# Seven-product pairs with the sums on VectorE and low parts of slabs by accumulating transfers

## The chip, the core and the metric

The kernel runs on one core of a Trainium2 chip. The engines that matter here are TensorE (PE, which multiplies, with PEld for its weight loads), VectorE (DVE), ScalarE (ACT), GpSimd (POOL) and SyncE (SP, which issues the loads). Each works through its own list of instructions in order and waits at semaphores for the others. The metric is the device time of one execution in microseconds.

## What is computed

One decoder layer over 512 tokens with 1024 features: half a feed-forward layer, a mixer of two recurrent branches, half a feed-forward layer, and a normalisation. All in float32.

```python
D_MODEL = 1024
SEQ = 512
D_FF = 2816

def swiglu(x, w_in, w_out):
    a, b = jnp.split(x @ w_in, 2, axis=-1)
    return (jax.nn.silu(a) * b) @ w_out

h = h + 0.5 * swiglu(rmsnorm(h, ffn1_norm[l]), ffn1_w_in[l], ffn1_w_out[l])
h = h + hybrid_mixer(rmsnorm(h, mix_norm[l]), ...)
h = h + 0.5 * swiglu(rmsnorm(h, ffn2_norm[l]), ffn2_w_in[l], ffn2_w_out[l])
```

The change touches the two feed-forward layers alone.

## The kernel before

**Three matmuls for one.** A product in full float32 precision is made of three matmuls in the faster float32r type: each operand is split into a rounded high part and the rest, the low part, and `mm3` (lines 166 to 169) adds high times high, high times low and low times high in PSUM. For a slab of weights (128x512, 256 KB) ACT casts the loaded tile to the high part `whi` (line 298), and DVE subtracts the high part from the tile to get the low part `wlo` (line 282).

**A stream of units.** A feed-forward layer is a list of units, one slab of 12 matmuls each, that `stream` lays out by hand, in the order in which each engine shall run them. After the matmuls of unit t it emits, for later units, the low part of unit t+5, the sums for unit t+8, the cast of unit t+6, and the loads for which a buffer has come free. `WB = 6` buffers hold high and low parts, so the cast for unit t+6 waits until PE is done with unit t. Raw slabs lie in three buffers `raw` or, in the stage described next, in six buffers `rw`; a count of readers (`left`) in the program tells when the next load may be put into SP's list (line 275).

**Pairs.** The hidden layer has 2816 columns, 22 blocks of 128. A pair is one block of `a` and the block of `b` that it is multiplied with. In the plain form a pair is eight products, four units of full-width matmuls (512 columns each; tiles `pmm`), two for `a` and two for `b`. In the seven-product form (`fast`, from line 315) the eight quarter products of the 2x2 blocked matrices are replaced by seven, in the scheme of Strassen and Winograd: seven units of half-width matmuls (256 columns; tiles `px`), of which three take a loaded tile as it is (`a11`, `a12`, `a22`), and four take a sum `sw` of loaded tiles (`s1` to `s4`, made at line 327 on POOL). The results come together on DVE in `fa`, `uu`, `uc` (line 346) and `vb` (line 362), ACT takes the silu, and the gate multiplies both halves (line 426). Results of the last five blocks are split again at once (lines 429 and 430).

**Before the stage** the normalised input has to be put into seven operands `xs` with high and low parts (`operands`, from line 387): eight scalings on DVE (line 399), four differences on POOL and DVE (line 398), seven casts on ACT (line 396) and seven low parts on DVE (line 397). They are spread over ten units from unit 2 (first layer) or 3 (second layer) on. PE meanwhile does pairs in the plain form: two in units 0 to 7 of the first layer, whose first two pairs are done in an opening, and three in units 0 to 11 of the second. So 18 and 19 of the 22 pairs are made in the seven-product form.

**Behind it** comes the output product, eight columns of six units each (`w2`), with the split of the gated blocks (lines 485 and 486) in its first column.

The mixer's order is made by a planner of its own and is not touched.

Of the kernel before, what the change touches and what calls it, by code (L numbers as in the profile page):

```python
# [8 lines left out]
F32 = mybir.dt.float32  # L9
# [3 lines left out]
ALU = mybir.AluOpType  # L13
# [3 lines left out]
P = 128  # L17
T = 512
NT = T // P
D = 1024  # L20
KD = D // P
# [18 lines left out]
WB = 6  # L40
RW, SW = 6, 4
# [84 lines left out]
def body(tc, xT, cst, sqc, hmask, dta, w1o, w1a, w2a, wt, wn, wab, wbh, wbg, wo, w1b, w2b, yT, dbg=None):  # L126
# [110 lines left out]
    class Unit:  # L237

        def __init__(self, raws, operand, run, comb=None, drop=()):
            self.raws, self.operand, self.run, self.comb, self.drop = raws, operand, run, comb, drop  # L240

    def plain(src, nk, xs, where, n=T):
# [3 lines left out]
        def unit(k):  # L246
# [9 lines left out]
            return Unit([raw], lambda: raw.tile[:, :w_ * P], run, drop=(raw,))  # L256
        return [unit(k) for k in range(0, nk, 4)], held

    def stream(units, fp, early, hooks, posts):
# [18 lines left out]
        def ahead(comb, cast, low):  # L278
            while todo["low"] < min(low, len(units)):
                i = todo["low"]  # L280
                x, hi, lo = parts[i]
                dve.tensor_tensor(lo, x, hi.bitcast(F32), op=ALU.subtract)  # L282
                for r in units[i].drop:
                    r.left -= 1
                todo["low"] += 1
# [6 lines left out]
            while todo["cast"] < min(cast, len(units)):  # L292
# [5 lines left out]
                act.copy(hi, x)  # L298
                parts[i] = x, hi, lo
# [6 lines left out]
        for t, u in enumerate(units):  # L306
# [5 lines left out]
            ahead(min(t, todo["cast"]) + WB + 3, min(t + WB + 1, todo["cast"] + 2), min(t + WB, todo["cast"]))  # L312
        assert not waiting

    def fast(w, p, xo, fp, at, posts, gate):
# [7 lines left out]
        def comb(n, x, y, op):  # L323
            def f():
                a, b = (z.tile if isinstance(z, Raw) else v[z] for z in (x, y))
                v[n] = fp.tile([P, T], F32, name="sw", bufs=SW)
                pool.tensor_tensor(v[n], a, b, op=op)  # L327
# [45 lines left out]
        for t, f in ((0, f0), (2, f2), (3, f3), (4, f4), (6, f6), (7, f7), (8, f8)):  # L373
# [5 lines left out]
            Unit([a11, a21], raw(a11), prod(0, 0, "m"), drop=(a11,)),  # L379
            Unit([a22, a12], of("s2"), prod(2, 0, "a"), lambda: (s1(), s2())),  # L380
            Unit([], raw(a12), prod(3, 1), drop=(a12,)),
# [3 lines left out]
            Unit([], raw(a22), prod(6, 0), drop=(a22,))]  # L385

    def operands(c0, xs, rooms, start, hooks):
# [4 lines left out]
              for o in range(7)]  # L392
# [8 lines left out]
        work = ((scaled(0), scaled(1)), (scaled(2), scaled(3), less(pool, t1, b12, b11)),  # L401
                (high(0), scaled(4), scaled(5)), (scaled(6), scaled(7), low(0)),
                (less(pool, b12, b22, b12), less(dve, t2, b22, t1), high(3), high(2)), (low(2), low(3), high(1)),
                (low(1), less(pool, t2, b21, t2), high(4)), (low(4), high(5)), (low(5), high(6)), (low(6),))
# [4 lines left out]
    def ffn(w1, w2, c0, after, slow, lead=None, last=None):  # L409

        with tc.tile_pool(name="ff", bufs=1) as fp, \
# [33 lines left out]
            if lead is not None:  # L445
# [4 lines left out]
                for p in range(2):  # L450
                    f = columns([lambda x=x: x for x in pts[2 * p:2 * p + 2]], ("fa", "uc"), p, *([pool, dve][p],) * 2)
# [7 lines left out]
            for p in range(done, slow):  # L459
                us = []  # L460
                for n in range(2):
                    x, held = plain(w1[ORDER[p], n], KD, ux, pa if lead is None and p == 0 else mm)
# [39 lines left out]
            for d in range(KD if last is None else KD - 1):  # L502
                x, held = plain(w2[d], KF, lambda k, d=d: go[k] if d < 2 else moved[k], mm)
# [125 lines left out]
    ffn(w1a, w2a, C_F1, nextnorm(C_MX, hd, defer=True), 4, lead=lead)  # L629
# [1304 lines left out]
```

## Time and profile before

| what | us |
|---|---|
| median of 3 runs | 1681.99 (1681.3 to 1683.33) |
| profiled execution | 1681.47 |
| its span, first to last instruction | 1679.7 |
| PE busy in the span | 1617.8 |
| DVE busy | 1266.9 |
| POOL busy | 572.0 |
| first layer, seven-product matmuls | 56.8 to 271.4 |
| second layer, seven-product matmuls | 1327.6 to 1543.4 |

The busy time of PE is modelled from the starts of pipelined matmuls, so a busy PE may still run below its best rate; the number of matmuls in a stretch tells that rate. A timeline row gives start, duration, engine, line, operation, output and inputs, and in brackets the idle time ahead of it with what ended that. Instructions of one engine overlap by some 0.08 us in the rows, so the time from start to start is a little shorter than the duration.

### The profile page before, as it was taken

How to read it: one execution, taken by the hardware profiler on the slowest of the kernel's cores; microseconds unless marked ns; L12 is line 12 of the kernel's file. 1: busy time of each engine (PE TensorE's matmuls, PEld its weight loads, DVE VectorE, ACT ScalarE, POOL GpSimd, SP SyncE). 2: the span in 40 equal slices, each digit the busy share in tenths (PEclk: the TensorE clock that was granted, in tenths of full speed). 3: DMA queues.
4: the chain of work that ended last, by engine and by line, in shares of the span. 5: the costliest groups of instructions: out<-in, count | busy, mean ns of one | idle time of the engine just before them, and what ended most of it. 6: DMA issues, size and time to landing. Idle time of an engine off the chain costs nothing.

```text
span 1679.7 us, 29400 instructions
## 1 busy us (share of the span) xinstructions
PE 1617.8 (96%) x10708; PEld 1395.8 (83%) x10708; DVE 1266.9 (75%) x2212; ACT 768.9 (46%) x1779; POOL 572.0 (34%) x782
## 2 busy tenths in 40 slices
PE   9799989999999999999999999999999899999997
PEld 8698988888888888887888888888888798988787
DVE  5999999345778859757889887755544999999534
ACT  5344446334335245536766565554234443445322
POOL 1655542000221212056617656600001655542001
PEclk9899999999999999999999999999999999999999
DMA  6133332334223223453334234445633233332333
GB/s 199 45 96 92 91 100 77 117 117 125 72 62 95 53 82 95 124 151 103 95 105 119 86 110 127 130 150 176 199 109 105 88 96 90 95 95 73 102 100 113
DMA packets 107425, 178.70 MB, mean 106 GB/s; under 512 B 19584, under 2 KB 25472, under 8 KB 107280
## 3 DMA queue, kind: packets, MB, share of 16 engines
q1 hardware_dynamic: 106992, 176.60, 35.3%
q8 instruction: 84, 1.38, 0.3%
q14 instruction: 61, 0.50, 0.1%
q10 hardware_dynamic: 288, 0.22, 0.0%
HBM read 161.80 MB, written 14.97 MB: 105 GB/s over the span
## 4 chain that ended last, share of the span: by engine, by line
PE 69%; DVE 24%; issue 4%; ACT 2%; DMA 1%; SPq 0%; POOL 0%; DVEq 0%; POOLq 0%; ACTq 0%
PE pmm L167 18%; PE pmm L169 17%; PE pmm L168 17%; DVE wlo L282 11%; DVE rooma L426 3%; DVE roomb L426 2%; PE pnat L167 2%; PE pnat L169 2%; PE pnat L168 2%; DVE uc L346 1%; DVE uu L346 1%; DVE fa L346 1%; DVE g L426 1%; DVE xs L397 1%; PE pog L1357 1%
## 5 line engine op out<-in xcount | busy, mean ns | idle before, releaser
L167 PE MATMUL pmm<-uh,whi 128*128 128x512 f32 (+1 forms) x863 | 358.6, 416 | 3.1 <-DVE uc L440 3.1
L169 PE MATMUL pmm<-uh,wlo 128*128 128x512 f32 (+1 forms) x863 | 337.8, 391 | 0.0
L168 PE MATMUL pmm<-ul,whi 128*128 128x512 f32 (+1 forms) x863 | 336.5, 390 | 0.0
L169 PE MATMUL px<-xs,wlo 128*128 128x256 f32 x1036 | 301.3, 291 | 30.1 <-DVE wlo L282 29.9
L167 PE MATMUL px<-xs,whi 128*128 128x256 f32 x1036 | 296.6, 286 | 7.9 <-DVE fa L440 4.2
L168 PE MATMUL px<-xs,whi 128*128 128x256 f32 x1036 | 296.6, 286 | 5.3 <-DVE xs L397 5.3
L1711 DVE TENSOR_TENSOR wlo<-raw,whi 128x512 fp32r<-128x512 f32 x226 | 157.9, 699 | 118.5 <-ACT whi L1709 116.9
L1709 ACT CAST whi<-raw 128x512 fp32r<-128x512 f32 x226 | 140.3, 621 | 224.7 <-PE pmm L168 177.4
L169 PEld LDWEIGHTS px<-xs,wlo 128*128 128x128 f32 x1036 | 201.7, 195 | 39.5 <-DVE wlo L282 39.3
L167 PEld LDWEIGHTS px<-xs,whi 128*128 128x128 f32 x1036 | 201.9, 195 | 8.9 <-ACT xs L396 6.3
L168 PEld LDWEIGHTS px<-xs,whi 128*128 128x128 f32 x1036 | 201.9, 195 | 6.4 <-DVE xs L397 6.4
L169 PEld LDWEIGHTS pmm<-uh,wlo 128*128 128x128 f32 x863 | 162.4, 188 | 36.0 <-DVE wlo L558 0.2
L167 PEld LDWEIGHTS pmm<-uh,whi 128*128 128x128 f32 x863 | 162.9, 189 | 33.2 <-issue 3.5
L168 PEld LDWEIGHTS pmm<-ul,whi 128*128 128x128 f32 x863 | 163.1, 189 | 28.6 <-DVE ul L194 0.3
L327 POOL TENSOR_TENSOR sw<-rw 128x512 f32<-128x512 f32 x74 | 120.4, 1627 | 151.0 <-DMA rw<-w1b 60.5
L282 DVE TENSOR_TENSOR wlo<-raw,whi 128x512 fp32r<-128x512 f32 x122 | 95.5, 797 | 88.6 <-ACT whi L298 88.1
L282 DVE TENSOR_TENSOR wlo<-sw,whi 128x512 fp32r<-128x512 f32 x148 | 146.8, 1010 | 0.0
L298 ACT CAST whi<-raw 128x512 fp32r<-128x512 f32 x122 | 71.7, 590 | 145.8 <-PE pmm L168 85.1
L205 POOL TENSOR_TENSOR acc<-acc,sqt 128x512 f32<-128x512 f32 x18 | 23.5, 1304 | 321.6 <-ACT sqt L203 321.6
L282 DVE TENSOR_TENSOR wlo<-rw,whi 128x512 fp32r<-128x512 f32 x111 | 97.6, 880 | 0.0
L167 PE MATMUL pmm<-xs,whi 128*128 128x512 f32 (+1 forms) x238 | 90.1, 379 | 3.0 <-ACT xs L485 3.0
L168 PE MATMUL pmm<-xs,whi 128*128 128x512 f32 (+1 forms) x238 | 90.2, 379 | 1.7 <-DVE xs L486 1.7
(478 smaller groups left out, 3315.6 us busy)
## 6 DMA issues: line engine op xcount, KB each, us to landing
raw<-wt SPq DMA_DIRECT2D x160, 256.0 KB
rw<-w1b SPq DMA_DIRECT2D x76, 256.0 KB
rw<-w1a SPq DMA_DIRECT2D x72, 256.0 KB
raw<-w2b SPq DMA_DIRECT2D x45, 256.0 KB
raw<-w2a SPq DMA_DIRECT2D x40, 256.0 KB
raw<-wn SPq DMA_DIRECT2D x32, 256.0 KB
raw<-wbg SPq DMA_DIRECT2D x32, 256.0 KB
gb<-gtd SPq DMA_DIRECT2D x16, 256.0 KB
```

The costliest lines, as they stand in the source:

```text
L167: pe.matmul(pt, ah, bh, start=first, stop=False)
L168: pe.matmul(pt, ah, bl, start=False, stop=False)
L169: pe.matmul(pt, al, bh, start=False, stop=last)
L205: add.tensor_tensor(acc, acc, s, op=ALU.add)
L282: dve.tensor_tensor(lo, x, hi.bitcast(F32), op=ALU.subtract)
L298: act.copy(hi, x)
L327: pool.tensor_tensor(v[n], a, b, op=op)
L346: dve.tensor_tensor(t2, p2, add.to_broadcast([P, 2, 256]) if twice else add, op=ALU.add)
L397: low = lambda o: lambda: dve.tensor_tensor(xo[o][1], what[o], xo[o][0].bitcast(F32), op=ALU.subtract)
L426: mul.tensor_tensor(g[:, c], x, y, op=ALU.mult)
L1709: act.copy(hi, raw)
L1711: dve.tensor_tensor(lo, raw, hi.bitcast(F32), op=ALU.subtract)
```

## The change

1. The four sums of a pair (`sw`) move from POOL to DVE, and so do POOL's three differences in `operands` and, in the first layer, the scaling and gate of the pair from the opening.
2. A unit may be marked `fold`. Its low part is then not made on DVE: ACT writes minus the high part into `wlo`, and POOL issues a transfer that reads the slab from memory a second time and adds it onto `wlo` on arrival. Marked are the three plain tiles of each seven-product pair, the units of the eight-product pairs from the fourth block of the first layer and the second of the second layer on, and the first output column of each layer.
3. The sums are emitted one unit later (`COMB = 2` where 3 stood).
4. The first layer makes one pair more in eight products (`slow` is 5, was 4), so 17 and 19 pairs are left in the seven-product form.

```diff
-RW, SW = 6, 4
+RW, SW, COMB = 6, 4, 2
...
-            return Unit([raw], lambda: raw.tile[:, :w_ * P], run, drop=(raw,))
+            return Unit([raw], lambda: raw.tile[:, :w_ * P], run, drop=(raw,), fold=raw.src if fold else None)
...
                 x, hi, lo = parts[i]
-                dve.tensor_tensor(lo, x, hi.bitcast(F32), op=ALU.subtract)
-                for r in units[i].drop:
-                    r.left -= 1
+                if units[i].fold is None:
+                    dve.tensor_tensor(lo, x, hi.bitcast(F32), op=ALU.subtract)
+                    for r in units[i].drop:
+                        r.left -= 1
                 todo["low"] += 1
...
                 act.copy(hi, x)
+                if units[i].fold is not None:
+
+                    act.mul(lo, hi.bitcast(F32), -1.0)
+                    pool.dma_start(lo, units[i].fold, accum_op=ALU.add)
+                    for r in units[i].drop:
+                        r.left -= 1
...
-            ahead(min(t, todo["cast"]) + WB + 3, min(t + WB + 1, todo["cast"] + 2), min(t + WB, todo["cast"]))
+            ahead(min(t, todo["cast"]) + WB + COMB, min(t + WB + 1, todo["cast"] + 2), min(t + WB, todo["cast"]))
...
-                pool.tensor_tensor(v[n], a, b, op=op)
+                dve.tensor_tensor(v[n], a, b, op=op)
...
-            Unit([a11, a21], raw(a11), prod(0, 0, "m"), drop=(a11,)),
+            Unit([a11, a21], raw(a11), prod(0, 0, "m"), drop=(a11,), fold=a11.src),
...
-        work = ((scaled(0), scaled(1)), (scaled(2), scaled(3), less(pool, t1, b12, b11)),
+        work = ((scaled(0), scaled(1)), (scaled(2), scaled(3), less(dve, t1, b12, b11)),
...
-                    f = columns([lambda x=x: x for x in pts[2 * p:2 * p + 2]], ("fa", "uc"), p, *([pool, dve][p],) * 2)
+                    f = columns([lambda x=x: x for x in pts[2 * p:2 * p + 2]], ("fa", "uc"), p, dve, dve)
...
-                    x, held = plain(w1[ORDER[p], n], KD, ux, pa if lead is None and p == 0 else mm)
+                    x, held = plain(w1[ORDER[p], n], KD, ux, pa if lead is None and p == 0 else mm, fold=p > (2 if lead is not None else 0))
...
-                x, held = plain(w2[d], KF, lambda k, d=d: go[k] if d < 2 else moved[k], mm)
+                x, held = plain(w2[d], KF, lambda k, d=d: go[k] if d < 2 else moved[k], mm, fold=d == 0)
...
-    ffn(w1a, w2a, C_F1, nextnorm(C_MX, hd, defer=True), 4, lead=lead)
+    ffn(w1a, w2a, C_F1, nextnorm(C_MX, hd, defer=True), 5, lead=lead)
```

What the engines' lists then hold. First DVE, one seven-product pair in the first layer, before (lines as in the profile; `x2` is a row that comes twice):

```order
L282 TENSOR_TENSOR wlo<-rw,whi 128x512
L346 TENSOR_TENSOR fa<-px,p_874 128x512
L282 TENSOR_TENSOR wlo<-rw,whi 128x512
L282 TENSOR_TENSOR wlo<-sw,whi 128x512
L346 TENSOR_TENSOR uu<-px,fa 128x512
L362 TENSOR_TENSOR vb<-px,uu 128x256
L282 TENSOR_TENSOR wlo<-rw,whi 128x512
L282 TENSOR_TENSOR wlo<-sw,whi 128x512
L346 TENSOR_TENSOR uc<-px,uu 128x512
L282 TENSOR_TENSOR wlo<-sw,whi 128x512 x2
L426 TENSOR_TENSOR roomb<-fa,uc 128x256
L426 TENSOR_TENSOR roomb<-uc,vb 128x256
```

And DVE in such a pair of the changed kernel, up to the first of the gate's two rows (later lines have moved by up to seven; L334 is the sum, L283 the low part, L353 and L369 the results, L433 the gate):

```order
L334 TENSOR_TENSOR sw<-rw 128x512
L334 TENSOR_TENSOR sw<-sw,rw 128x512
L353 TENSOR_TENSOR fa<-px,p_1268 128x512
L283 TENSOR_TENSOR wlo<-sw,whi 128x512
L353 TENSOR_TENSOR uu<-px,fa 128x512
L369 TENSOR_TENSOR vb<-px,uu 128x256
L334 TENSOR_TENSOR sw<-rw 128x512
L283 TENSOR_TENSOR wlo<-sw,whi 128x512
L334 TENSOR_TENSOR sw<-rw,sw 128x512
L353 TENSOR_TENSOR uc<-px,uu 128x512
L283 TENSOR_TENSOR wlo<-sw,whi 128x512 x2
L433 TENSOR_TENSOR rooma<-fa,uc 128x256
```

The three low parts of loaded tiles are gone, and four sums stand in their places; each sum is for a unit of the next pair.

ACT in the same pair before, from the silu of `uc` to the next:

```order
L368 ACTIVATE uc<-uc 128x256
L351 COPY p_874<-px 128x256
L298 CAST whi<-rw 128x512 x2
L298 CAST whi<-sw 128x512
L357 ACTIVATE fa<-fa 128x256
L298 CAST whi<-rw 128x512
L298 CAST whi<-sw 128x512 x3
```

And in the changed kernel (L302 writes minus the high part):

```order
L375 ACTIVATE uc<-uc 128x256
L358 COPY p_970<-px 128x256
L299 CAST whi<-rw 128x512
L302 ACTIVATE wlo<-whi 128x512
L299 CAST whi<-rw 128x512
L302 ACTIVATE wlo<-whi 128x512
L299 CAST whi<-sw 128x512
L364 ACTIVATE fa<-fa 128x256
L299 CAST whi<-rw 128x512
L302 ACTIVATE wlo<-whi 128x512
L299 CAST whi<-sw 128x512 x3
```

Each cast of a loaded tile is followed by the product by -1 that starts from it.

POOL at the start of the first layer, in the changed kernel (before, its list held the sums of L327 here, four a pair):

```order
L230 ISA
L230 TENSOR_TENSOR rcol<-msq,mhalf 128x4
L303 DMA wlo<-w1a 128x512 x59
L303 DMA wlo<-w2a 128x512 x5
L303 DMA wlo<-w2a 128x256
L508 CAST roomb<-uh 128x512
```

POOL issues 65 transfers in the first layer (8 for eight-product pairs, 51 for 17 seven-product pairs, 6 for the output column) and nothing else between the norm and the copies behind the first output column.

14 lines of the change are left out of this document (7 added, 7 removed).

## The prediction

> **What bounds the kernel now.** I first read the page: busy shares and the 40 slices (42 us each).
>
> ```profile
> PE 1617.8 (96%) x10708; PEld 1395.8 (83%) x10708; DVE 1266.9 (75%) x2212; ACT 768.9 (46%) x1779; POOL 572.0 (34%) x782
> ...
> DVE  5999999345778859757889887755544999999534
> ...
> POOL 1655542000221212056617656600001655542001
> PEclk9899999999999999999999999999999999999999
> ```
>
> PE at 96% hides two stretches, slices 2 to 7 and 32 to 37, where DVE stands at 9 and POOL works beside it: the seven-product stages of the two feed-forward layers. Next the same stretch by windows (PE, PEld, DVE, ACT, POOL busy, then clock, DMA share and GB/s).
>
> ```profile
> core 0: us, PE busy (x) PEld busy (x) DVE busy (x) ACT busy (x) POOL busy (x), PEclk, DMA share, GB/s
> 40.00:60.00 20.00, 15.47 (x68) 12.72 (x66) 19.51 (x17) 4.87 (x8) 13.61 (x7) 0.90 0.14 44
> 60.00:80.00 20.00, 13.61 (x76) 12.53 (x77) 19.45 (x18) 10.56 (x17) 12.12 (x6) 0.76 0.17 51
> 80.00:100.00 20.00, 20.00 (x167) 19.88 (x166) 19.96 (x24) 8.25 (x18) 10.76 (x8) 1.00 0.31 83
> 100.00:120.00 20.00, 19.12 (x159) 18.86 (x157) 19.93 (x23) 8.64 (x19) 12.38 (x8) 1.00 0.31 92
> 0.00:20.00 20.00, 18.95 (x84) 15.97 (x85) 14.30 (x25) 15.30 (x27) 0.20 (x4) 1.00 0.79 259
> 108.00:109.00 1.00, 0.93 (x8) 0.73 (x7) 1.00 (x1) 0.00 (x0) 0.87 (x1) 1.00 0.45 133
> 109.00:110.00 1.00, 0.19 (x1) 0.19 (x2) 1.00 (x3) 0.00 (x0) 0.00 (x0) 1.00 0.34 129
> ```
>
> From 80 us on DVE has no gap (19.93 of 20), while PE loses almost a microsecond at 109. Before that, at 40 to 80 us, PE stands idle for 11 us and its clock drops to 0.76. So VectorE sets the pace. Third, DVE in order of time over one pair, and what POOL does then (start, duration):
>
> ```profile
> 109.07 0.68 DVE L282 TENSOR_TENSOR wlo<-rw,whi 128x512 fp32r<-128x512 f32 x1
> 109.67 0.68 DVE L346 TENSOR_TENSOR fa<-px,p 128x512 f32<-128x512 f32 x1
> ...
> 112.19 0.42 DVE L362 TENSOR_TENSOR vb<-px,uu 128x256 f32<-128x256 f32 x1
> 112.53 0.68 DVE L282 TENSOR_TENSOR wlo<-rw,whi 128x512 fp32r<-128x512 f32 x1
> 113.13 1.79 DVE L282 TENSOR_TENSOR wlo<-sw,whi 128x512 fp32r<-128x512 f32 x1
> ...
> 117.42 1.52 DVE L426 TENSOR_TENSOR roomb<-fa,uc 128x256 f32<-128x256 f32 x1
> 118.86 1.51 DVE L426 TENSOR_TENSOR roomb<-uc,vb 128x256 f32<-128x256 f32 x1
> 120.29 0.68 DVE L282 TENSOR_TENSOR wlo<-rw,whi 128x512 fp32r<-128x512 f32 x1
> ...
> 265.81 0.42 DVE L426 TENSOR_TENSOR g<-fa,uc 128x256 f32<-128x256 f32 x1
> ```
>
> ```profile
> 112.52 1.85 POOL L327 TENSOR_TENSOR sw<-rw 128x512 f32<-128x512 f32 x1 [3.65 <-DMA rw<-w1a]
> ...
> 116.97 1.68 POOL L327 TENSOR_TENSOR sw<-rw 128x512 f32<-128x512 f32 x1 [0.63 <-DVE wlo L282]
> ```
>
> A pair takes 120.29 - 109.07 = 11.22 us. The same 128x512 subtraction takes 0.68 us (0.60 from start to start) without POOL and 1.79 us beside POOL's sum; the 128x256 product of the gate takes 1.52 us beside POOL and 0.42 us (0.34 from start to start) at 265.81, after POOL's last sum. DVE is full because POOL's reads hold up its instructions with two SBUF inputs.
>
> **The change, part by part.** *DVE in the steady pair.* Three subtractions go, four sums come, and POOL's reads end. Left are 11 instructions of 128x512 at 0.60 and three of 128x256 at 0.34: 6.6 + 1.0, and 0.1 for the wait between `uu` and `vb`, 7.7 us in place of 11.22. The sums have two SBUF inputs as the subtractions do, so I take 0.60; were they as slow as beside POOL (1.79) DVE would need 12.5, which gives 1613 + 36 x 2.4 = 1700 us by the sum below. I keep that as the far end, though nothing is left that would make them so.
>
> *PE is then late next.* Its spacing from rows:
>
> ```profile
> 37.91 0.39 PE L169 MATMUL pmm<-uh,wlo 128*128 128x512 f32 x1
> ...
> 52.19 0.39 PE L169 MATMUL pmm<-uh,wlo 128*128 128x512 f32 x1
> 56.79 0.55 PE L167 MATMUL px<-xs,whi 128*128 128x256 f32 x1 [4.22 <-DVE fa L440]
> ...
> 82.08 0.28 PE L167 MATMUL px<-xs,whi 128*128 128x256 f32 x1
> ...
> 84.00 0.28 PE L168 MATMUL px<-xs,whi 128*128 128x256 f32 x1
> ...
> 1292.10 1.05 PE L221 MATMUL pbc<-sq,rcol 128*128 128x128 f32 x8
> ```
>
> 64 full-width matmuls from 37.91 up to 52.42 give 0.227 us each, so a unit of 12 takes 2.72 and an eight-product pair (48) 10.88; 16 half-width ones from 82.08 to 84.00 give 0.120, so a unit takes 1.44 and a seven-product pair (84) 10.08. The ends of both stages:
>
> ```profile
> L169 PE MATMUL px<-xs,wlo x504: 278/283/582, 57.4 to 271.3; 128*128 128x256 f32 x168
> L169 PE MATMUL px<-xs,wlo x532: 277/283/581, 1328.0 to 1543.3; 128*128 128x256 f32 x178
> ```
>
> First layer: the eight-product pairs end at 52.42 and the stage of 18 pairs at 271.42. With one pair more in eight products: 52.42 + 10.88 + 17 x 10.08 = 234.7, a gain of **36.7 us**. Second layer: unit 2 starts behind the `pbc` matmuls, at 1292.10 + 1.05 = 1293.2; ten units later, at 1320.4, the 19 pairs could start, and end at 1511.9 in place of 1543.4: **31.5 us**.
>
> *Operands ahead of the stage* (40 to 80 us). Three POOL subtractions move to DVE. Rows for what DVE does there:
>
> ```profile
> 53.50 1.41 DVE L399 SCALAR_TENSOR_TENSOR rooma<-h,cs,rbc 128x512 f32<-128x512 f32 x2
> 54.83 1.22 DVE L397 TENSOR_TENSOR xs<-rooma,xs 128x1024 fp32r<-128x1024 f32 x1
> ```
>
> Eight scalings at 0.67, four differences and seven low parts at 1.14 are 17.9 us. With pair results (1.8 a pair), sums and lows I count about 29 us on DVE, in 29 us of PE work in the first layer (the added pair is its cover) and 27 in the second. The overhang of 2 is work that later units need, so I cost it at nothing; uncovered it is up to 3 us a layer. The lower clock goes with the idle time.
>
> *ACT.* It gains three products by -1 a pair.
>
> ```profile
> 104.34 0.42 ACT L368 ACTIVATE uc<-uc 128x256 f32<-128x256 f32 x1 [2.67 <-DVE uc L346]
> 104.66 0.36 ACT L351 COPY p<-px 128x256 f32<-128x256 f32 x1
> 104.91 1.15 ACT L298 CAST whi<-rw 128x512 fp32r<-128x512 f32 x2
> ```
>
> A cast alone is 0.62 (1.15 for two): 7 casts at 0.53, 3 products at 0.62, silus and copy 1.0 make 6.6 of 10.08, hidden by PE. In the first output column of each layer six products (3.7 us) come into a PE stretch of 15 us, while six subtractions leave DVE; I take zero, with 0 to 4 us a layer as its bounds. The rest of the kernel issues what it issued.
>
> *The wait that is added.* PE now waits in three units of seven for an accumulating transfer, which waits on POOL behind nothing but other such transfers. A slab's buffers come free when the unit six earlier is done. From that end: the copy to `p` (0.25), cast (0.62), product (0.62) and three handoffs of 0.1 (an estimate), 1.8 us; then X, the transfer with its issue by POOL; then the unit's last ten matmuls (1.2) and one unit (1.44) close a loop of seven units. So a pair takes at least 4.44 + X, and X is free up to 5.6 us. The trace has no transfer issued by POOL and none that accumulates. The nearest rows are plain loads of the same 256 KB:
>
> ```profile
> 107.47 0.33 SPq L275 DMA_DIRECT2D rw<-w1a  x1
> 109.78 0.33 SPq L275 DMA_DIRECT2D rw<-w1a  x1
> ```
>
> The first moves its 262 KB between 108 and 110 us; the second is on hand when POOL's sum begins at 112.52, 2.7 us after its issue. Low end X = 2.7. High end: the destination is fetched like a second load, 5.4, and POOL is busy as long as with a tile, 1.7: X = 7.1, where a pair takes 11.5 us. I take the middle, 4.9, which is free. A transfer that meets a load (four bursts of 1.2 us in 10.08, so about half of them) I let come 1.2 us later: X = 6.1, a pair of 10.54, 0.46 over, for half of 36 pairs: **8 us** lost.
>
> The Trainium skill (DMA: Bandwidth & Descriptors, Anatomy of one DMA) prices a transfer issued by GpSimd at 2.0 us and bytes over 436 GB/s, an estimate of 2.6 us here; by it the 8 us would fall away. No run shows such a transfer yet.
>
> DVE's sums also wait for loads now, in DVE's own queue: behind `s1` stand `fa` and a low part. The third load of a pair is asked for when `s3` frees its buffer and needed four units (5.8 us) later; at 2.7 us it is on hand, and DVE has 2.3 us to spare besides.
>
> **Sum**, against the profiled execution's 1681.47 us (span 1679.7 and 1.8 around it; the median of the three runs, 1681.99, is 0.03% away): 1681.5 - 36.7 - 31.5 + 8 = **1621 us**.
>
> **Rivals.** *Late transfers.* The wait on PE takes the place of DVE's fullness: at X = 7.1 the loss is 36 x 1.46 = 53 us on 1613, **1666 us**. For it: the loop has only 0.7 us of room over my middle value. Against: half that bound is a guess that POOL is as slow with an issue as with a tile.
>
> *Transfers fill the DMA engines: slower.* At the start 259 GB/s move, so a load costs 1.01 us of all engines and four of them 4.04 a pair. If an accumulation costs c, a pair cannot be shorter than 4.04 + 3c. The gain is gone at 1613 + 36 x 1.9, a pair of 11.98, so from c = 2.65 us on. At three loads' worth (3.03) a pair takes 13.1 and the time is 1613 + 36 x 3.05 = **1723 us**. For it: fetch, fetch of the destination and write-back may not overlap. Against: shares of 0.31 leave two thirds of the engines unused.
>
> The Trainium skill (DMA: Bandwidth & Descriptors, Rules for kernel authors) says that an accumulation reads its destination and writes it later. Counted as two loads, c = 2.02 and a pair needs 10.1, level with PE: by that rule the forecast stands, but with no room left.
>
> *DVE stays the bound*, because its long rows are its own and not POOL's doing: 11.22 less three subtractions plus four sums is 11.8 us, 36 x 1.74 on 1613: **1676 us**. Against it stands the gate's 0.42 at 265.81.
>
> **How the numbers follow.** Forecast (1606 to 1640): 0.52. Late transfers (to 1672): 0.22. DVE still the bound (1672 to 1685): 0.05, of which 0.03 within 0.2% (about what a measurement can tell from no change). Slower: 0.18. Below 1606, where the output stages gain too: 0.03. Range 1606 to 1700, up to the far end of the sums' price; it leaves out that 0.03 and most of the slower cases. Faster 0.79, same 0.03, slower 0.18.
>
> **What the new profile would show.** Right: DVE at 7 to 8 tenths in the stages, gate rows of 0.42, sums of 0.68, PE without gaps at 40 to 80 us and some 165 matmuls in 20 us. Late transfers: PE waits for `wlo` by DMA in units 0, 2 and 6 of a pair. Full engines: a DMA share near 1 there, and DVE's sums waiting for `rw`. Wrong altogether if DVE rows stay at 1.5 us.

## The result and the profile after

The changed kernel takes **1624.2 us** (median; 1623.3 to 1625.1 in four runs) where the kernel before took 1682.7 in the same sitting. The ratio is **0.965**, with a 95% interval of 0.964 to 0.967. The forecast was 1621.

The page of the kernel after, first its span and busy shares, then rows of the 40 slices (40.5 us each):

```profile
span 1621.5 us, 29531 instructions
...
PE 1599.9 (99%) x10672; PEld 1386.6 (86%) x10672; DVE 1129.2 (70%) x2223; ACT 865.5 (53%) x1910; POOL 440.8 (27%) x761
...
DVE  5877776446787779758889888755544788787433
...
POOL 1122223001221222156617666510002222222001
PEclk9999999999999999999999999999999999999998
DMA  6788875333312222453334233445544688887433
```

In the two stages DVE has come down from 9 tenths to 7 and 8, POOL from 5 or 6 to 2, and the DMA engines have gone up to 8. The same stretches by windows (PE, PEld, DVE, ACT, POOL busy, the clock granted to PE as a share of full speed, DMA share, GB/s):

```profile
core 0: us, PE busy (x) PEld busy (x) DVE busy (x) ACT busy (x) POOL busy (x), PEclk, DMA share, GB/s
40.00:60.00 20.00, 17.32 (x70) 13.89 (x70) 14.25 (x19) 10.88 (x17) 4.09 (x6) 0.91 0.90 216
80.00:100.00 20.00, 19.32 (x161) 19.12 (x160) 15.41 (x28) 13.50 (x26) 5.19 (x6) 1.00 0.85 188
120.00:140.00 20.00, 20.00 (x169) 20.00 (x169) 16.02 (x29) 13.98 (x27) 5.21 (x6) 1.00 0.87 184
```

The count of matmuls tells most. At 120 to 140 us PE starts 169 in 20 us, one every 0.118 us: its own rate. At 80 to 100 it starts 161, so 8 of them (0.95 us) are lost though PE counts as busy for 19.32. At 40 to 60 it idles for 2.7 us.

DVE's groups between 80 and 240 us (busy us, mean ns, then idle time before them):

```profile
L283 DVE TENSOR_TENSOR wlo<-sw,whi 128x512 fp32r<-128x512 f32 x62 | 41.1, 685 | 1.0
L334 DVE TENSOR_TENSOR sw<-rw 128x512 f32<-128x512 f32 x30 | 20.6, 687 | 5.8 <-DMA rw<-w1a 5.8
...
L433 DVE TENSOR_TENSOR rooma<-uc,vb 128x256 f32<-128x256 f32 x8 | 3.4, 419 | 0.0
```

The long rows are gone: low parts of sums take 685 ns on the mean, the sums themselves 687 and the gate 419, where the trace before had rows of 1790 and 1520 beside POOL.

The stage itself, by the last of the three matmuls of each product, first layer and second (min, median and max ns, first and last start):

```profile
L169 PE MATMUL px<-xs,wlo x476: 278/283/388, 67.9 to 244.5; 128*128 128x256 f32 x159
...
L169 PE MATMUL px<-xs,wlo x532: 277/283/387, 1292.1 to 1487.2; 128*128 128x256 f32 x178
```

and PE's waits in it for the added transfers (us in total, times, longest):

```profile
PE px L169 <- DMA wlo<-w1a: 3.4, 8, 0.7
...
PE px L169 <- DMA wlo<-w1b: 2.4, 4, 1.4
```

The first matmul of the stage starts at 67.6 (1291.8 in the second layer), and 17 pairs end at 244.6, 19 at 1487.3: 10.41 and 10.29 us a pair, in place of 11.2 and more. In time gained, from the two traces:

| stretch | before | after | gained | forecast |
|---|---|---|---|---|
| start to end of layer 1's pairs | 271.4 | 244.6 | 26.8 | 32.9 |
| from there to the start of layer 2's `pbc` matmuls | 1020.7 | 1019.1 | 1.6 | 0 |
| from there to the end of layer 2's pairs | 251.3 | 223.6 | 27.7 | 27.3 |
| from there to the end of the span | 136.3 | 134.2 | 2.1 | 0 |
| sum | 1679.7 | 1621.5 | 58.2 | 60.2 |

(The forecast's 8 us for late transfers are shared out over 17 and 19 pairs.) The second layer went as forecast. The first is 6.1 us short, and the output columns and what lies beyond gave 3.7 that were not counted.

Where the first layer lost, in the timeline (start, duration; in brackets the idle time before and what ended it), first PE, then DVE, then ACT:

```profile
49.70 0.76 PE L167 MATMUL pmm<-uh,whi 128*128 128x512 f32 x1 [2.68 <-DVE uc L447]
50.26 0.63 PE L168 MATMUL pmm<-ul,whi 128*128 128x512 f32 x1
50.69 0.63 PE L169 MATMUL pmm<-uh,wlo 128*128 128x512 f32 x1
...
45.68 0.69 DVE L433 TENSOR_TENSOR roomb<-fa,uc 128x512 f32<-128x512 f32 x1 [6.38 <-ACT fa L449]
...
43.31 0.62 ACT L299 CAST whi<-raw 128x512 fp32r<-128x512 f32 x1 [3.84 <-DMA raw<-w1a]
...
44.51 0.62 ACT L449 ACTIVATE g<-g 128x512 f32<-128x512 f32 x1
45.03 1.14 ACT L449 ACTIVATE fa<-fa 128x512 f32<-128x512 f32 x2
```

It is read from the bottom: a cast waits 3.84 us for its load, the silus stand behind it in ACT's list, DVE's gate waits 6.38 us for the silu, DVE's `uc`, which frees the PSUM bank, comes late, and PE waits 2.68 us for that bank. The mean clock of that window is 0.91: in steps of 2 us it reads 0.88, 0.50 and 0.76 from 48 to 54 us, with the wait and just behind it, and 1.00 on both sides. The matmuls behind the wait start 0.43 us apart at first, not 0.23. Together this puts PE some 4.5 us behind its pace before the wait (an estimate from these starts), which covers the 4.3 us by which the stage starts later than forecast (67.6, not 63.3).

The added transfer itself, in the page's parts on groups, queues and issues:

```profile
q1 hardware_dynamic: 106992, 176.60, 35.6%
q0 software_dynamic: 19584, 35.40, 14.7%
...
L303 POOL DMA_DIRECT2D wlo<-w1b x65 | 56.4, 878 | 164.1 <-ACT wlo L302 137.6
...
wlo<-w1b POOLq DMA_DIRECT2D x65, 256.0 KB, 4.9
```

and in the timeline, from the product by -1 on ACT to the issue on POOL:

```profile
102.12 0.63 ACT L302 ACTIVATE wlo<-whi 128x512 fp32r<-128x512 f32 x1
...
103.04 0.86 POOL L303 DMA_DIRECT2D wlo<-w1a  x1 [5.29 <-ACT wlo L302]
```

The product ends at 102.75, POOL issues at 103.04, and a transfer lands 4.9 us after its issue (median). From the end of the product that is 5.2 us, where the forecast had 5.0 (a handoff of 0.1 and an X of 4.9).

### The profile page after: what moved, and what is told of

Read it like the earlier page. It is cut to its first block, busy times and chain, and to the rows that moved or that the text cites. A ratio compares the mean times of both kernels' runs of the same rounds, so it can differ in the third digit from the quotient of the medians.

```text
span 1621.5 us, 29531 instructions
## 1 busy us (share of the span) xinstructions
PE 1599.9 (99%) x10672; PEld 1386.6 (86%) x10672; DVE 1129.2 (70%) x2223; ACT 865.5 (53%) x1910; POOL 440.8 (27%) x761
## 3 DMA queue, kind: packets, MB, share of 16 engines
q1 hardware_dynamic: 106992, 176.60, 35.6%
q0 software_dynamic: 19584, 35.40, 14.7%
## 4 chain that ended last, share of the span: by engine, by line
PE 90%; DMA 4%; issue 2%; DVE 2%; ACT 1%; POOL 1%; POOLq 0%; SPq 0%; ACTq 0%; DVEq 0%
PE pmm L167 19%; PE pmm L169 19%; PE pmm L168 19%; PE px L169 6%; PE px L168 5%; PE px L167 5%; DMA wlo<-w1a 2%; PE pnat L167 2%; PE pnat L169 2%; PE pnat L168 2%; DMA wlo<-w1b 1%; PE pog L1364 1%; PE pgq L1150 1%; PE pw L1348 1%; PE pl L935 1%
## 5 line engine op out<-in xcount | busy, mean ns | idle before, releaser
L167 PE MATMUL pmm<-uh,whi 128*128 128x512 f32 x879 | 365.0, 415 | 2.7 <-DVE uc L447 2.7
L169 PE MATMUL pmm<-uh,wlo 128*128 128x512 f32 x879 | 344.0, 391 | 2.2 <-DMA wlo<-w2a 1.1
L168 PE MATMUL pmm<-ul,whi 128*128 128x512 f32 x879 | 342.6, 390 | 0.0
L167 PE MATMUL px<-xs,whi 128*128 128x256 f32 x1008 | 285.2, 283 | 0.0
L168 PE MATMUL px<-xs,whi 128*128 128x256 f32 x1008 | 285.2, 283 | 0.0
L1718 DVE TENSOR_TENSOR wlo<-raw,whi 128x512 fp32r<-128x512 f32 x226 | 158.8, 703 | 118.3 <-ACT whi L1716 116.7
L299 ACT CAST whi<-sw 128x512 fp32r<-128x512 f32 x144 | 89.3, 620 | 88.8 <-DVE sw L334 78.5
L283 DVE TENSOR_TENSOR wlo<-raw,whi 128x512 fp32r<-128x512 f32 x98 | 75.9, 789 | 82.3 <-ACT whi L299 81.9
L303 POOL DMA_DIRECT2D wlo<-w1b x65 | 56.4, 878 | 164.1 <-ACT wlo L302 137.6
L283 DVE TENSOR_TENSOR wlo<-sw,whi 128x512 fp32r<-128x512 f32 x144 | 95.8, 685 | 2.4
L303 POOL DMA_DIRECT2D wlo<-w1a x59 | 51.2, 868 | 156.8 <-ACT wlo L302 129.8
L167 PE MATMUL pmm<-xs,whi 128*128 128x512 f32 (+1 forms) x238 | 89.8, 377 | 0.0
```

What stands on the lines that cost most here:

```text
L167: pe.matmul(pt, ah, bh, start=first, stop=False)
L168: pe.matmul(pt, ah, bl, start=False, stop=False)
L169: pe.matmul(pt, al, bh, start=False, stop=last)
L303: pool.dma_start(lo, units[i].fold, accum_op=ALU.add)
L1718: dve.tensor_tensor(lo, raw, hi.bitcast(F32), op=ALU.subtract)
```

## The experiments

The theory after the result: the gain comes from taking POOL's arithmetic away; the accumulating transfers are a separate matter, which relieves DVE at the price of a wait on PE. The rival: both are needed, since DVE would be too full for the sums without the transfers. Each run was timed beside the kernel before; ratios are against it.

### The sums alone, and the transfers alone

First the kernel before with all of POOL's sums, differences and gates put on DVE, nothing else:

```diff
-                pool.tensor_tensor(v[n], a, b, op=op)
+                dve.tensor_tensor(v[n], a, b, op=op)
...
(so in less(pool, ...) of operands and in the opening's gate)
```

> The kernel before with one part of the change alone: all of POOL's sums, differences, the scaling and the gate in the feed-forward layers go to DVE; no accumulating transfer, four pairs before the stage, sums emitted as before. Theory (POOL's reads hold up DVE): a pair costs DVE 14 x 0.60 + 0.1 + 3 x 0.34 = 9.5 us, under PE's 10.08; the ten late blocks some 0.7 us over. Gate rows 0.42 us; time 1615 to 1635. Rival (DVE's instruction count is what limits, POOL does not matter): four sums more make 11.2 + 2.4 = 13.6 us a pair, time about 1770.

Measured: 1635.6 us, ratio 0.974 (0.972 to 0.975), just above the expected range (1615 to 1635). Its windows:

```profile
40.00:60.00 20.00, 13.35 (x46) 10.46 (x46) 15.94 (x25) 6.01 (x10) 0.00 (x0) 0.74 0.24 77
80.00:100.00 20.00, 20.00 (x169) 20.00 (x169) 19.86 (x36) 10.06 (x20) 0.00 (x0) 1.00 0.33 106
```

From 80 us on PE runs at its own rate, 169 matmuls, although DVE has four sums more and hardly a gap. DVE's low parts of sums take 683 ns here, with POOL idle and every low part still on DVE. What is missing is lost before: at 40 to 60 us PE starts 46 matmuls, with one wait of 6.6 us for DVE, and the clock falls to 0.74; at 60 to 80 us it waits another 5.7 us for the operands.

Then the reverse: the kernel after, with the four sums of a pair back on POOL (and emitted as early as before), the transfers kept.

```diff
-                dve.tensor_tensor(v[n], a, b, op=op)
+                pool.tensor_tensor(v[n], a, b, op=op)
```

> The changed kernel with the four sums of a pair back on POOL, emitted as before the change; the accumulating transfers stay. Theory: DVE has 4.7 us of its own and is held up for some 4, so it falls under PE's 10.08, but the transfers stand behind sums of 1.5 us in POOL's list, so X grows from 5.2 to 6.2 to 6.9 and a pair takes 10.7 to 11.3 us: 1635 to 1660, with PE waiting for wlo by transfer. Rival (moving the sums is a side matter, the transfers alone bring the gain): 1624 within 4.

Measured: 1664.5 us, ratio 0.990 (0.988 to 0.991), 4.5 us above the expected range. DVE's groups and POOL's between 80 and 240 us:

```profile
L283 DVE TENSOR_TENSOR wlo<-sw,whi 128x512 fp32r<-128x512 f32 x57 | 88.9, 1578 | 3.1 <-ACT whi L299 3.0
...
L334 POOL TENSOR_TENSOR sw<-rw 128x512 f32<-128x512 f32 x28 | 46.0, 1644 | 32.7 <-DMA rw<-w1a 22.1 <-DVE wlo L283 7.7 <-DVE uc L353 2.9
L303 POOL DMA_DIRECT2D wlo<-w1a x43 | 39.4, 982 | 12.7 <-DVE vb L369 5.9 <-ACT wlo L302 4.7 <-DVE wlo L283 1.9
```

The same low part of a sum takes 1578 ns on the mean in place of 685 (before the change 1069, with rows of 0.68 and 1.79 us), and apart from the earlier emission only POOL's sums were put back: its issues were there in both. This bears out the forecast's reason for DVE's long rows. The Trainium skill (SBUF — State Buffer, Who interferes with whom) has it as a rule: a VectorE instruction with two SBUF inputs contends with a GpSimd instruction that reads SBUF. These two runs agree, 1578 against 685 ns. Here DVE is no longer full throughout (16.3 of 20 us at 120 to 140), and PE waits for transfers, which now stand behind sums in POOL's list: 28 us of PE's waits are for `wlo` by DMA, and a pair takes 11.4 and 11.1 us.

### Everything but the transfers, and the transfers in one place only

The kernel after with no accumulating transfer at all:

```diff
-            Unit([a11, a21], raw(a11), prod(0, 0, "m"), drop=(a11,), fold=a11.src),
+            Unit([a11, a21], raw(a11), prod(0, 0, "m"), drop=(a11,)),
...
(so for a12 and a22, for the eight-product pairs and for the first output column)
```

> The changed kernel without any accumulating transfer: all low parts on DVE again; sums on DVE, five pairs before the first stage, sums emitted one unit later. Theory: 9.5 us of DVE a pair, so PE still sets the pace and no wait for a transfer is left: 1613 to 1630, level with the change or a little better. Rival (the gain needs the transfers, since DVE at 9.5 of 10.08 in list order loses time at every wait): 1640 or more.

Measured: 1625.9 us, ratio 0.968 (0.966 to 0.969): the interval overlaps that of the kernel after (0.964 to 0.967). Two windows:

```profile
120.00:140.00 20.00, 20.00 (x169) 20.00 (x168) 19.39 (x35) 10.09 (x20) 0.00 (x0) 1.00 0.33 107
240.00:260.00 20.00, 17.22 (x75) 13.04 (x74) 18.86 (x33) 14.38 (x28) 2.24 (x3) 0.91 0.32 86
```

The pairs take 10.08 and 10.14 us: without a transfer nothing is lost in them, and DVE holds the pace (by the forecast's own count, 7.7 us and three low parts at 0.60 make 9.5 of 10.08). But the stage starts at 71.2 us, not 67.6, and at 240 to 260 us, at the first output column, PE idles for 2.8 us. So the transfers, taken together, lose in the pairs and gain ahead of them and behind them, about as much. The next runs tell which of them does what.

Next only in the seven-product pairs (none ahead of the stage, none in the output column):

```diff
-                    x, held = plain(w1[ORDER[p], n], KD, ux, pa if lead is None and p == 0 else mm, fold=p > (2 if lead is not None else 0))
+                    x, held = plain(w1[ORDER[p], n], KD, ux, pa if lead is None and p == 0 else mm, fold=False)
...
-                x, held = plain(w2[d], KF, lambda k, d=d: go[k] if d < 2 else moved[k], mm, fold=d == 0)
+                x, held = plain(w2[d], KF, lambda k, d=d: go[k] if d < 2 else moved[k], mm)
```

> The changed kernel with accumulating transfers in the seven-product pairs alone; eight-product pairs and the output column get their low parts from DVE. Theory (the first layer's stage starts at 67.6 us and not at 63.3 because loads for the eight-product pairs stand behind twice as heavy transfers and ACT's silu stands behind such a load): the stage starts 3 to 5 us earlier, 1618 to 1622. Rival (DVE needs that relief there): 1626 or more.

Measured: 1625.7 us, ratio 0.968 (0.966 to 0.969). The pairs stay at 10.34 and 10.28 us. But the stage starts at 71.3 us where 62.6 to 64.6 was expected, and the time is not the expected 1618 to 1622: a miss. I had held the start's delay to be the transfers' doing; without them there it is worse, since DVE then has the low parts of the eight-product pairs to make besides the operands (PE waits for it three times, for 1.7 to 2.0 us). At the first output column, which has no transfers here either, nothing is lost: from the end of layer 2's pairs to the end of the span it is 132.8 us, against 134.2 in the kernel after and 137.8 in the run without any transfer.

The complement, transfers in the eight-product pairs and in the first output column alone:

```diff
-            Unit([a11, a21], raw(a11), prod(0, 0, "m"), drop=(a11,), fold=a11.src),
+            Unit([a11, a21], raw(a11), prod(0, 0, "m"), drop=(a11,)),
...
(so for a12 and a22)
```

> The changed kernel with accumulating transfers where DVE is short (eight-product pairs and first output column) and none in the seven-product pairs. Theory (in the pairs the transfers only add a wait, ahead of them they relieve DVE): pairs at 10.08 to 10.15 us as without transfers, first stage starting at 67 to 68 us as with them: 1612 to 1618, faster than both. Rival (DVE, fuller in the first pairs, gives the start back): 1622 or more.

Measured: 1620.2 us, ratio 0.964 (0.962 to 0.965), 2 us above the expected range. Pairs of 10.08 us in both layers and a start at 68.1, as expected. PE's longest waits:

```profile
PE pmm L167 <- DVE uc L447: 3.0, 1, 3.0
PE pmm L169 <- DMA wlo<-w2b: 2.5, 1, 2.5
PE pmm L169 <- DMA wlo<-w2a: 2.5, 1, 2.5
```

What remains is one wait at the start and one at each first output column, this one for a transfer. From the end of layer 2's pairs to the end of the span it is 137.0 us, hardly less than without any transfer: the column's own transfers don't make up for those that are gone from the pairs.

The same with the first layer's transfers in the fifth pair only:

```diff
-                    ... fold=p > (2 if lead is not None else 0))
+                    ... fold=p > (3 if lead is not None else 0))
```

> As the last, but in the first layer the transfers begin with the fifth pair and not the fourth, so that four of them are gone while the first loads come in. Theory (the 43 us wait of ACT for a load is queueing behind transfers): the first stage starts at 64 to 67 us, 1610 to 1616. Rival (DVE is short of those four low parts): the stage starts at 69 or later, 1617 or more.

Measured: 1619.2 us, ratio 0.963 (0.962 to 0.964), no different from the run before and above the expected 1610 to 1616. The start is 67.7 us where 64 to 67 was expected: fewer transfers on the way do not bring it forward. So something else holds it.

### How long a transfer is free

The loop of the forecast says that a transfer is free while 4.44 + X stays under 10.08 us. So the cast, and with it the transfer, was put one unit (1.44 us) nearer to its use, in the kernel after and in the one without transfers:

```diff
-            ahead(min(t, todo["cast"]) + WB + COMB, min(t + WB + 1, todo["cast"] + 2), min(t + WB, todo["cast"]))
+            ahead(min(t, todo["cast"]) + WB + COMB - 1, min(t + WB, todo["cast"] + 2), min(t + WB - 1, todo["cast"]))
```

> The changed kernel with casts, sums and low parts of a stream emitted one unit later, so that the cast for unit t+5 and not t+6 follows unit t (the number of buffers stays). Theory (the loop of a cast, product, transfer and PE sets a floor for a pair): one unit less of lead raises the floor from 4.44 + X to 5.88 + X, with X = 5.2 from 9.6 to 11.1 us a pair, 0.7 to 1.0 more than the 10.35 it takes now: 1648 to 1662. Rival (PE's waits for transfers are scattered collisions with loads, and the loop has room): 1634 or less.

> The same shift by one unit in the kernel without accumulating transfers. Theory: a low part from DVE is there some 2 us after the cast, so a unit less of lead costs nothing in the pairs: 1624 to 1636. Rival (a shorter lead hurts whatever makes the low part, since DVE is full to 9.5 of 10.08): 1645 or more.

Measured: 1641.2 us, ratio 0.976 (0.975 to 0.977), with transfers; 1626.1 us, ratio 0.967 (0.966 to 0.968), without. With transfers the pairs grow to 10.97 and 10.74 us, by 0.56 and 0.45; the expected 0.7 to 1.0 was too much, and the time lies between theory (1648 to 1662) and rival (1634 or less). But PE's waits for `wlo` by DMA grow from 5.8 to 16.1 us. Without transfers the time stays; the pairs there grow by 0.19 and 0.17 us, as DVE's low parts have less lead as well (PE waits 3.8 us for them), and the earlier start at 66.2 us makes up for it. So what the lead does to the transfers alone is 0.37 and 0.28 us a pair: a shorter lead costs, as the loop says, and less than its 1.44 us, since the loop had room before. The pairs stay below the 11.1 that was worked out with X = 5.2; that X holds the handoff ahead of the issue, which the loop's 4.44 counts already. With the 4.9 from issue to landing the loop gives 10.8, near what was measured.

An accident of the run with transfers told more: its stage starts at 62.8 us, and at 40 to 60 us PE has no gap at all. One unit less of lead takes the silus out from behind the cast that waits for its load.

### The late start

So the shorter lead was given to the first eight units of layer 1 alone:

```diff
-            ahead(min(t, todo["cast"]) + WB + COMB, min(t + WB + 1, todo["cast"] + 2), min(t + WB, todo["cast"]))
+            b = WB - (t < near)
+            ahead(min(t, todo["cast"]) + b + COMB, min(t + b + 1, todo["cast"] + 2), min(t + b, todo["cast"]))
...
-            stream(units, fp, 3, hooks, posts)
+            stream(units, fp, 3, hooks, posts, 8 if lead is not None else 0)
```

> The kernel after, with one line of the stream changed: for the first eight units of layer 1 alone the lookahead of casts and low parts is one unit shorter, everywhere else as it is. Theory (layer 1's seven-product stage begins 4 to 5 us late because ACT's silu stands in its list behind a cast that waits for a load): the row of PE at 49.70 us that waits 2.68 us for VectorE's uc goes or falls under 1 us, the stage begins at 62.5 to 64.5 us in place of 67.6, pairs stay at 10.41 and 10.29 us, and the time falls by 3 to 5 us to 1619 to 1621 us. Rival (the start is late because VectorE has too much to do there, whatever the order in ACT's list): the stage begins at 66.5 us or later and the time stays at 1622.5 us or above.

Measured: 1619.3 us, ratio 0.963 (0.962 to 0.965). The stage starts at 63.4 us (PE's wait for `uc` is gone), and ACT's timeline shows the silu first and the waiting cast behind it:

```profile
40.63 0.62 ACT L450 ACTIVATE fa<-fa 128x512 f32<-128x512 f32 x1
44.46 0.62 ACT L299 CAST whi<-raw 128x512 fp32r<-128x512 f32 x1 [3.21 <-DMA raw<-w1a]
```

The cast still waits 3.2 us for its load, but now nothing that DVE or PE needs stands behind it. The pairs are nearly unchanged (10.45 and 10.32). The theory held for the start, by 4.2 us. (The shorter lead moves DVE's low parts and sums as well; but in the trace after DVE stood idle for 6.38 us for that silu, so its own order was not what held the start.) Of the time this much is less firm: the medians differ by 4.9 us, but the two intervals overlap, and in the profiled executions 3.6 us of it are left at the end of layer 1's pairs, 2.0 at layer 2's `pbc` matmuls and 0.9 in the span.

And what the fifth eight-product pair is for, the kernel after with four:

```diff
-    ffn(w1a, w2a, C_F1, nextnorm(C_MX, hd, defer=True), 5, lead=lead)
+    ffn(w1a, w2a, C_F1, nextnorm(C_MX, hd, defer=True), 4, lead=lead)
```

> The kernel after with four eight-product pairs in layer 1, as before, in place of five. It tells what the fifth is for. Theory (VectorE prepares the seven-product operands during the eight-product pairs and needs the time of the fifth): the seven-product stage begins about 10.9 us earlier in the list, at 56 to 57 us if nothing waits, but waits for its operands; 18 pairs of 10.4 us follow; losses of 2 to 8 us show as PE waiting for DVE at the stage's start, and the time is 1625 to 1632 us. Rival (nothing waits, the fifth pair only costs its eighth product: 10.88 less 10.08 us): 1623.0 to 1624.0 us, and no wait of PE for DVE over 1 us beyond those of the kernel after.

Measured: 1631.6 us, ratio 0.970 (0.969 to 0.972). The stage begins at 54.5 us but PE waits there for operands that are not made yet:

```profile
58.37 0.38 PE L167 MATMUL px<-xs,whi 128*128 128x256 f32 x1 [2.19 <-ACT xs L403]
59.63 0.58 PE L168 MATMUL px<-xs,whi 128*128 128x256 f32 x1 [0.88 <-DVE xs L404]
...
66.58 0.39 PE L168 MATMUL px<-xs,whi 128*128 128x256 f32 x1 [0.91 <-DVE xs L404]
```

Its 18 pairs end at 247.2, against 244.6 for 17 pairs and the added one: the added pair is cover for the operands, as the forecast had it.

### Two that put the findings together

The shorter lead, transfers in the eight-product pairs and in the last two seven-product pairs of each layer, none in the others and none in the output column:

```diff
-            Unit([], raw(a12), prod(3, 1), drop=(a12,), fold=a12.src),
+            Unit([], raw(a12), prod(3, 1), drop=(a12,), fold=a12.src if p >= KF - 2 else None),
...
-                x, held = plain(w2[d], KF, lambda k, d=d: go[k] if d < 2 else moved[k], mm, fold=d == 0)
+                x, held = plain(w2[d], KF, lambda k, d=d: go[k] if d < 2 else moved[k], mm)
```

> The same shorter lookahead in layer 1's first eight units, and accumulating transfers only where the runs so far saw VectorE behind: in the eight-product pairs and in the last two seven-product pairs of each layer; the other seven-product pairs and the first output column have their low parts on VectorE. Theory (two separate losses, the late start and the wait in the pairs, add up): stage start at 62.5 to 64.5 us, pairs of 10.08 to 10.15 us, the first output product waits less than the 2.5 us of the run with transfers in eight-product pairs alone, time 1610 to 1616 us. Rival (VectorE at 19 to 20 of 20 us in the pairs has no slack, so what is gained at the start is lost again before or at the output columns): 1618 to 1624 us, with VectorE's waits of 2 us or more still in the list of what held TensorE.

Measured: **1612.4 us, ratio 0.959 (0.957 to 0.960)**, the best of all. The start is 63.4 us; the pairs take 10.25 and 10.20, more than the 10.15 expected, nearly all of it lost in the last two pairs; the first output column waits 0.19 us. Its windows:

```profile
200.00:220.00 20.00, 18.62 (x154) 18.21 (x152) 18.45 (x33) 12.26 (x25) 1.99 (x3) 1.00 0.47 111
220.00:240.00 20.00, 19.48 (x153) 19.07 (x154) 17.01 (x29) 13.94 (x27) 3.19 (x4) 1.00 0.58 134
240.00:260.00 20.00, 19.81 (x87) 15.94 (x86) 17.52 (x27) 12.03 (x23) 8.33 (x10) 1.00 0.42 119
```

Are those last transfers worth their price? The same without them:

> The kernel with the shorter lookahead in layer 1's first eight units, and accumulating transfers in the eight-product pairs alone: compared with the last run but one, the six transfers of the last two seven-product pairs of each layer are gone, too. That run's pairs lost 2.7 and 2.3 us, all but about 0.5 us of it in those last two pairs of each layer, where TensorE waited for the low part by transfer (two waits of about 1 us a layer). Theory (a transfer in a seven-product pair only costs, and VectorE needs no relief ahead of the output product): pairs of 10.08 to 10.12 us in both layers, waits of TensorE at the first output column under 0.5 us, time 1606.5 to 1609 us. Rival (those transfers buy VectorE the time that it needs for the first output column): the same pairs, but a wait of 2 us or more at the first output column of each layer, and 1611 to 1614 us.

Measured: 1616.1 us, ratio 0.961 (0.959 to 0.963). The rival's mechanism held, though the time is 2 us above its range. The pairs fall to 10.09 and 10.08 us as expected, but at the first output column PE now waits:

```profile
246.47 0.50 PE L167 MATMUL pmm<-xs,whi 128*128 128x512 f32 x1 [1.25 <-ACT xs L493]
247.88 0.58 PE L168 MATMUL pmm<-xs,whi 128*128 128x512 f32 x1 [0.92 <-DVE xs L494]
```

and its window from 240 to 260 us has 66 matmuls at a clock of 0.91, where the run with them has 87 at 1.00; in layer 2, from 1480 to 1500 us, it is 68 at 0.91 against 91 at 1.00. A transfer late in the stage costs PE up to 1.1 us at a wait, and buys DVE the time to have the gated blocks ready when the output product asks for them. The intervals overlap by a hair, the ranges of the two do not (1611.1 to 1614.7, 1615.4 to 1617.9; the kernel before, timed beside each, differs by 0.6), and the traces show both sides of the trade.

The last column is the time from the end of layer 2's pairs to the end of the span (136.3 us before):

| kernel | us | ratio to before | start | us a pair | behind |
|---|---|---|---|---|---|
| after | 1624.2 | 0.964 to 0.967 | 67.6 | 10.41, 10.29 | 134.2 |
| sums alone (18 pairs in layer 1) | 1635.6 | 0.972 to 0.975 | 62.5 | 10.55, 10.12 | 136.7 |
| transfers alone (sums back on POOL) | 1664.5 | 0.988 to 0.991 | 71.5 | 11.4, 11.1 | 133.8 |
| no transfers | 1625.9 | 0.966 to 0.969 | 71.2 | 10.08, 10.14 | 137.8 |
| transfers in pairs only | 1625.7 | 0.966 to 0.969 | 71.3 | 10.34, 10.28 | 132.8 |
| transfers outside pairs only | 1620.2 | 0.962 to 0.965 | 68.1 | 10.08, 10.08 | 137.0 |
| the same, fewer in layer 1 | 1619.2 | 0.962 to 0.964 | 67.7 | 10.09, 10.09 | 136.9 |
| shorter lead everywhere | 1641.2 | 0.975 to 0.977 | 62.8 | 10.97, 10.74 | 134.1 |
| shorter lead, no transfers | 1626.1 | 0.966 to 0.968 | 66.2 | 10.27, 10.31 | 135.1 |
| one eight-product pair less (18 pairs) | 1631.6 | 0.969 to 0.972 | 54.5 | 10.70, 10.30 | 133.2 |
| shorter lead at the start | 1619.3 | 0.962 to 0.965 | 63.4 | 10.45, 10.32 | 134.6 |
| that, transfers only ahead and at the end | 1612.4 | 0.957 to 0.960 | 63.4 | 10.25, 10.20 | 132.6 |
| that, transfers only ahead | 1616.1 | 0.959 to 0.963 | 63.3 | 10.09, 10.08 | 137.4 |

Every run with transfers in the last pairs of the stage has 132.6 to 134.6 us behind it, every run without them 135.1 to 137.8.

## Why the forecast was right, and where it was not

**DVE's long rows are POOL's doing: right.** 685 and 419 ns after, 683 with POOL's work moved and nothing else, 1578 with POOL's sums put back. The rival that DVE stays the bound falls with it, and so does the far end at which the sums themselves would be slow (687 ns).

**PE is late next, at 10.08 us a pair: right.** Runs without transfers in the pairs show exactly that; the count of 169 matmuls in 20 us is the same thing.

**The added wait: right in kind, nearly in size.** From issue to landing a transfer took the 4.9 us that I had put in the middle between two bounds, so that this number was hit is partly luck; the pairs lost 5.6 + 4.0 = 9.6 us for the 8 that I took. The rival of late transfers (1666 us) needed X = 7.1; the longest in the pairs took 6.3. The rival of full DMA engines fails on its price: an accumulating transfer takes 14.7% of 1621.5 us over 136 transfers, 1.75 us of all engines, and a plain load of 256 KB takes 35.6% over 674 loads' worth (the queue's few stores counted in), 0.86: c counts 2.04 loads, not three. The Trainium skill (DMA: Bandwidth & Descriptors, Rules for kernel authors) says that an accumulation reads its destination and writes it later; a price of about two loads agrees with that, though no row here shows the reading itself. The forecast's 1.01 us for a load was too much: it took 259 GB/s for full engines, where the same row has their share at 0.79. At the measured prices a pair needs 4 x 0.86 + 3 x 1.75 = 8.7 us of the DMA engines, and the share of 0.85 to 0.87 in the stage is high but not full. What makes single transfers late can be read in part: between 100 and 210 us PE waits for four transfers, each of which took 6.1 to 6.3 us to land (the median there is 4.8) though POOL had been idle for 0.3 us when it issued it. So POOL's list is not what made them late; whether it was a load or the transfer issued 1.2 us before was not separated.

**Operands ahead of the stage: right in the second layer, wrong in the first.** In the second layer the stage starts 27.0 us after the `pbc` matmuls, as forecast (27.2). In the first it starts 4.3 us late, and the sign of PE without gaps at 40 to 80 us failed there. The step that was wrong is the one on ACT: it added up ACT's busy time in a seven-product pair, 6.6 of 10.08 us, and called it hidden, and the operands' step counted DVE's work alone. Neither asked what stands *behind* a cast that waits for a load. The run with the shorter lead took that one order away and got 4.2 us back at the start.

**The first output column: better than zero.** It cost PE 1.1 us of waiting in each layer, and still these stretches came out 1.6 and 2.1 us shorter than before. The column's own transfers did not do that: with them gone and those of the pairs kept, the stretches are 0.9 and 1.4 us shorter still. It is the transfers in the pairs that gain there: with none in the pairs the two stretches take 2.4 and 2.8 us longer (transfers outside pairs only). The last two runs show how, with the column's transfers gone: without those of the last two pairs PE waits for the split of the gated blocks on ACT and DVE.

**What the forecast did not see at all** is that its two parts were not both needed in the pairs. Its own count has DVE at 7.7 us, and at 9.5 without a transfer: both are under PE's 10.08. So inside the stage the three transfers of a pair could only lose; what they gain, they gain behind it, and the last two pairs' transfers are enough for that. I priced the change as a whole and never asked what each half gives alone: the sums with the fifth pair and no transfer give 1625.9 us, the transfers without the sums 1664.5.

**That the total came within 3 us is in part luck.** The first layer's shortfall of 6.1 us was partly made up by 3.7 us in stretches that the forecast had put at nothing.

## What to carry to other kernels

Take the engine that reads SBUF beside DVE out of the loop before lightening DVE: here moving work *onto* the full engine made it faster. Count a pair of changes apart, each against the engine that is late next, and spend a costly relief only where that engine really has to wait (here ahead of a stage and at its end, not inside it). And where a list is run in order, don't add up busy times alone: look for what stands behind an instruction that waits for a transfer.

## What the runs showed of the hardware

An accumulating transfer of 256 KB issued by POOL holds POOL for 0.87 us (982 ns beside POOL's own sums), lands 4.9 us after its issue (median) in stages with a DMA share of mostly 0.8 to 0.9, and takes as much of the DMA engines as 2.04 plain loads. The Trainium skill (DMA: Bandwidth & Descriptors, Anatomy of one DMA) gives 2.0 us and bytes over 436 GB/s, an estimate of 2.6 us for this size; the runs show nearly twice that. How much of the rest is the destination's reading and how much the busy engines was not separated.

POOL's issues do not hold DVE up: with some six of them in 20 us, DVE's instructions with two SBUF inputs keep their 685 and 419 ns, where the run without any has 683 for low parts of sums.

Short waits of PE can go with a lower clock behind them, but their length alone does not tell when. A single wait of 2.7 us (after, at 49.70) stands in a window with a granted clock of 0.91, and so do four waits of 2.7 us together within some 6 us (the last run, 240 to 260 us); 46 matmuls in 20 us went with 0.74 (the sums alone). In the run with transfers outside the pairs only, PE waits 2.5 us at the first output column of each layer: the window of the first, 240 to 260 us, has a clock of 1.00, that of the second, 1480 to 1500 us, 0.91. In the run with fewer of these in layer 1, a wait of 2.3 us at the start (40 to 60 us) went with 0.91, and one of 2.7 us at 240 to 260 us with 1.00. What decides, these runs don't show.
